# A decoder layer on one core: the second feed-forward's first product by seven quarter products per tile

## The chip, the cores and the metric

The kernel runs on one core of a Trainium2 chip. The metric is the time of one execution on the device in microseconds (us). Before the change it is 1444.54 us, the median of 3 runs (1444.05 to 1444.94).

## The reference

One decoder layer for 512 tokens of width 1024, in fp32. The change touches its last line alone:

```python
def swiglu_ffn(h, w_in, w_out):
    a, b = jnp.split(h @ w_in, 2, axis=-1)
    return (jax.nn.silu(a) * b) @ w_out

x = x + 0.5 * swiglu_ffn(rmsnorm(x, ffn1_norm_g), ffn1_w_in, ffn1_w_out)
# h = rmsnorm(x); sparse attention, gated convolution and attention into 256 memory tokens;
# their gated sum through a product with w_out is added to x
x = x + 0.5 * swiglu_ffn(rmsnorm(x, ffn2_norm_g), ffn2_w_in, ffn2_w_out)
```

The inner width is 2816, so w_in is 1024 x 5632 and w_out 2816 x 1024.

## The kernel before, in words

x is held transposed, xT: 8 blocks of 128 features on the partitions, 512 tokens in the columns. TensorE multiplies in fp32r. To keep fp32's accuracy every operand is split into a high and a low half, and each product is three matmuls into one PSUM bank, hi*hi, lo*hi and hi*lo (`mm3`, L237). In the feed-forward the 128 x 128 weight block is the stationary operand and 512 tokens move.

Stages: the first feed-forward, the attention, convolution and memory stages, the product with w_out of the layer, then the second feed-forward (`tail`, L1204, calls `ffn`, L301). `ffn` goes through 22 tiles of 128 inner features. A tile is two units of 24 matmuls (8 blocks of x by three), one for a into bank "g", one for b into "o". VectorE (DVE) and ScalarE (ACT) apply the token scale R = 1/rms, since x goes into the product unnormalized, then the gate: tanh on ACT, the rest on DVE, and split the result into ghi and glo. After 8, 15 and 22 tiles come eight units with w_out, which add into xT.

`Weights` (L95) delivers the weights. A unit is at most 128 x 1024; SP issues its transfer into one of three `wraw` buffers, and ACT (L130, cast to hi) and DVE (L131, the remainder lo) split it in two halves, each half ahead of its use. A raw buffer is free when its second half is split, and then SP issues the next transfer. Each engine takes its instructions in the order of its own queue. The order in the code is the program's, and a scheduler at build time moves instructions of DVE, ACT and PE within their dependences, and chooses which free buffer a tile gets.

Of the kernel before, what the change touches and what calls it, by code (L numbers as in the profile page):

```python
# [23 lines left out]
FFN_GROUPS = ((0, 8), (8, 15), (15, 22))  # L24
# [6 lines left out]
RAW_BUFS = 3  # L31
LINE = 256
PAD_LEFT, PAD_RIGHT = 128, 224
LOOK = 1
# [8 lines left out]
TOK["w"] = (256, (4, 4))  # L43

# [49 lines left out]

class Weights:  # L95


    def __init__(self, nc, pool, units):
        self.nc, self.pool, self.units = nc, pool, units
        self.i = self.i_dma = self.i_split = 0  # L100
        self.raw, self.parts = {}, {}

    def _dma(self, part=None):
        j = self.i_dma
        ap, _ = self.units[j]
        if part != 1:
            n = ap.shape[1]
            self.raw[j] = (self.pool.tile([128, 1024], F32, tag="wraw", name=f"wraw{j}", bufs=RAW_BUFS), n)
        t, n = self.raw[j]
        c = slice(0, n) if part is None else slice(512 * part, 512 * part + 512)  # L110
        self.nc.sync.dma_start(t[:, c], ap[:, c])
        if part != 0:
            self.i_dma += 1

    def _half(self):

        j = self.i_split
        t, n = self.raw[j]
        if j not in self.parts:
            hi = self.pool.tile([128, 1024], F32R, tag="whi", name=f"whi{j}", bufs=LOOK + 1)  # L120
            lo = self.pool.tile([128, 1024], F32R, tag="wlo", name=f"wlo{j}", bufs=LOOK + 1)
            self.parts[j] = (hi, lo)
            c = slice(0, min(n, 512))
        else:
            c = slice(512, n)
        if c.stop == n:
            self.raw.pop(j)
            self.i_split += 1
        hi, lo = self.parts[j]
        self.nc.scalar.copy(hi[:, c], t[:, c])  # L130
        self.nc.vector.tensor_sub(lo[:, c], t[:, c], hi[:, c].bitcast(F32))  # L131
        self.prefetch()

    def prefetch(self):
        while self.i_dma < len(self.units) and self.i_dma < self.i_split + RAW_BUFS:
            self._dma()

    def use(self, key):

        assert self.units[self.i][1] == key, (self.units[self.i][1], key)  # L140
        self.prefetch()
        while self.i_split <= self.i:
            self._half()
        self.i += 1
        self.ahead()
        return self.parts[self.i - 1]

    def ahead(self):

        self.parts.pop(self.i - 2, None)  # L150
        if self.i_split < len(self.units) and self.i_split <= self.i + LOOK - 1:
            self._half()


class Layer:
    def __init__(self, ctx, tc, ins, out, dbg=None):
# [10 lines left out]
        self.ws = Weights(nc, self.wp, self.unit_list())  # L167
# [16 lines left out]
    def unit_list(self):  # L184
        i = self.ins
        u = []

        def ffn(n):
            for gi, (f0, f1) in enumerate(FFN_GROUPS):
                for f in range(f0, f1):  # L190
                    for ab in range(2):
                        u.append((i[f"w{n}i"][f, ab], (n, "in", f, ab)))
                for m in range(NK):
                    u.append((i[f"w{n}o"][m][:, f0 * 128:f1 * 128], (n, "out", gi, m)))

        ffn("f1")
        for c in range(4):
            for q in range(4):
                u.append((i["wmkv"][c, q], ("mkv", c, q)))
        def tok(n, qs):  # L200
            for q in qs:
                u.append((i["t" + n][q][:, :TOK[n][0] * TOK[n][1][q]], ("tok", n, q)))

        def w1(kind, qs):
            for q in qs:
                u.append((i["w1" + "kv"[kind]][q], ("w1", kind, q)))
# [12 lines left out]
        u.append((i["w2k"], ("w2", 0)))  # L219
# [4 lines left out]
        u.append((i["w2v"], ("w2", 1)))  # L224
# [3 lines left out]
        for p in range(8):  # L228
            for t in range(6):
                u.append((i["wfeat"][p, t], ("feat", p, t)))  # L230
        for m in range(NK):
            u.append((i["wout"][m], ("wout", m)))
        ffn("f2")
        return u
# [66 lines left out]
    def ffn(self, key, pool, xhi, xlo, R, done, before, extra=()):  # L301
# [3 lines left out]
        nc = self.nc  # L305
        ghi = pool.tile([128, 8, 512], F32R, tag="ghi", name=self.nm("ghi"))
        glo = pool.tile([128, 8, 512], F32R, tag="glo", name=self.nm("glo"))
        def up(f, ab):
            whi, wlo = self.ws.use((key, "in", f, ab))
            p = self.ps("go"[ab])  # L310
            for k in range(NK):
                if k == NK // 2:
                    self.ws.ahead()
# [13 lines left out]
        for gi, (f0, f1) in enumerate(FFN_GROUPS):  # L327
            nf = f1 - f0
            for f in range(f0, f1):
                p = up(f, 0)  # L330
                if f > 0:
                    a = act_a(p)
                p2 = up(f, 1)
                if f == 0:
                    before()
                    a = act_a(p)
                nc.vector.tensor_tensor(a, a, p2, op=ALU.mult)  # L337
                self.split(ghi[:, f - f0], glo[:, f - f0], a)
                if 0 < f <= len(extra):
                    extra[f - 1]()  # L340
            for m in range(NK):
                whi, wlo = self.ws.use((key, "out", gi, m))
                p = self.ps("s")
                for k in range(nf):
                    if k == NK // 2:
                        self.ws.ahead()
                    c = slice(k * 128, (k + 1) * 128)
                    self.mm3(p, whi[:, c], wlo[:, c], ghi[:, k], glo[:, k], k == 0, k == nf - 1)
                if gi < len(FFN_GROUPS) - 1:
                    nc.vector.scalar_tensor_tensor(self.xT[:, m], p, 0.25, self.xT[:, m], op0=ALU.mult, op1=ALU.add)  # L350
                else:
                    done(m, p)


    def run(self):
# [41 lines left out]
        for k in range(NK):  # L397
            self.split_scaled(self.Ahi[:, k], self.Alo[:, k], self.xT[:, k], self.small[:, C_G1 + k:C_G1 + k + 1])
            if k in (0, 3):
                self.ws._half()  # L400
# [15 lines left out]
        self.ffn("f1", fp, self.Ahi, self.Alo, R, x1_done, x_rstd,  # L416
# [142 lines left out]
    def tok_chunk(self, c, evac):  # L559
# [4 lines left out]
        def quantum(q, tb):  # L564
# [4 lines left out]
            elif tb == 2:  # L569
                self.ws.ahead()  # L570
# [11 lines left out]
    def stage_b(self, memkv, prep, kfin):  # L582
# [20 lines left out]
        def evac_qm(half):  # L603
            def f(tb, p):
                nc.scalar.copy(mtok[:, tb, half * 512:half * 512 + 512], p)
                for h in (2 * half, 2 * half + 1):
                    sq = m1.tile([128, 256], F32, tag="qsq", name=self.nm("qsq"))
                    nc.scalar.activation(sq, mtok[:, tb, h * 256:(h + 1) * 256], AF.Square,
# [150 lines left out]
    def compress(self, cp, kcv, kind):  # L759
# [69 lines left out]
        def second():  # L829
            p = self.ps("t")  # L830
            hhi, hlo = st["h"]
            whi, wlo = (w.rearrange("p (k c) -> p k c", k=8) for w in self.ws.use(("w2", kind)))
# [371 lines left out]
    def tail(self, mx1):  # L1204
# [11 lines left out]
        f2 = ExitStack()  # L1216
        fp = self.pool(f2, "fp2", "left")
        xhi = fp.tile([128, NK, S], F32R, name="x2hi")
        xlo = fp.tile([128, NK, S], F32R, name="x2lo")
        acc = fp.tile([128, 512], F32, tag="acc", name="acc3")  # L1220
        for m in range(NK):
# [8 lines left out]
            self.prep_post(fp, m, self.xT[:, m], C_G2, xhi, xlo, acc)  # L1230
# [7 lines left out]

        def y_done(m, p):
            y = fp.tile([128, 512], F32, tag="y", name=self.nm("y"), bufs=2)  # L1240
# [3 lines left out]
        self.ffn("f2", fp, xhi, xlo, R, y_done, x_rstd)  # L1244
# [83 lines left out]
```

## Time and profile before

| | |
|---|---|
| median of 3 runs | 1444.54 us |
| profiled execution | 1445.14 us |
| its span, first to last instruction | 1443.4 us |
| PE busy | 1431.8 us (99%), 6915 matmuls |
| DVE busy | 887.8 us (62%) |
| ACT busy | 631.5 us (44%) |
| second feed-forward on PE | 1078.72 to 1439.5 us of the span |

PE is TensorE's matmuls, PEld its weight loads. Times inside the trace count from the span's start. Busy times of PE are overlapped: a matmul's shown duration is longer than its distance from the next one, so the length of a run of matmuls is read from starts.

### The profile page before, as it was taken

Reading aid. Unit: us, or ns where it says so; the run is one execution under the profiler, and the core shown is the slowest. Engines: PE = TensorE matmul, PEld = TensorE weight load, DVE = VectorE, ACT = ScalarE, POOL = GpSimd, SP = SyncE. Lnnn points to the kernel's source line nnn. Section 1 sums busy time; section 2 is a strip of 40 time slices with the busy share of each in tenths; the row PEclk is TensorE's granted clock in tenths of the full one; section 3 lists DMA queues with packets and bytes.
Section 4 is the critical chain, followed back from the end, with each engine's and each line's share of the span. In section 5 each row is a group of like instructions: output and inputs, shape, how many; then the busy total and the mean of one; then the engine's idle time right before and its main releaser. Section 6 shows DMA issues by size and latency. Waiting matters only on the chain.

```text
span 1443.4 us, 18864 instructions
## 1 busy us (share of the span) xinstructions
PE 1431.8 (99%) x6915; PEld 1198.8 (83%) x6915; DVE 887.8 (62%) x2120; ACT 631.5 (44%) x1455; POOL 1.3 (0%) x8
## 2 busy tenths in 40 slices
PE   9999999999999999999999999999999999999998
PEld 7888888888888789888888888888888888888887
DVE  7463554554766576678887887887665543543543
ACT  5242232233556645565655666565543322322331
POOL 0000000000000000000000000000000000000000
PEclk9999999999999999999999999999999999999999
DMA  5733333333452431222222222222233333333332
GB/s 179 247 123 102 97 87 101 97 96 91 149 169 92 125 94 59 89 94 68 74 75 80 67 82 74 66 74 74 73 93 97 90 100 101 90 90 110 91 93 97
DMA packets 42892, 142.62 MB, mean 99 GB/s; under 512 B 4704, under 2 KB 4992, under 8 KB 42672
## 3 DMA queue, kind: packets, MB, share of 16 engines
q1 hardware_dynamic: 40320, 134.83, 30.0%
q10 hardware_dynamic: 2480, 6.60, 1.3%
q8 instruction: 54, 0.88, 0.3%
q14 instruction: 38, 0.31, 0.1%
HBM read 139.27 MB, written 7.51 MB: 102 GB/s over the span
## 4 chain that ended last, share of the span: by engine, by line
PE 97%; DVE 1%; ACT 1%; DMA 0%; issue 0%; SPq 0%; ACTq 0%
PE psg L240 15%; PE psg L241 15%; PE psg L242 15%; PE pso L240 8%; PE pso L242 8%; PE pso L241 8%; PE pss L241 6%; PE pss L242 6%; PE pss L240 6%; PE pst L1044 2%; PE pso L1068 1%; PE pss L1002 1%; PE pss L1001 1%; PE pso L1067 1%; PE pst L969 1%; DMA xT<-xT 0%
## 5 line engine op out<-in xcount | busy, mean ns | idle before, releaser
L130 ACT CAST whi<-wraw 128x512 fp32r<-128x512 f32 (+1 forms) x492 | 279.5, 609 | 564.9 <-issue 324.1
L131 DVE TENSOR_TENSOR wlo<-wraw,whi 128x512 fp32r<-128x512 f32 (+1 forms) x492 | 315.1, 674 | 68.6 <-ACT whi L130 68.0
L240 PE MATMUL psg<-Ahi,whi 128*128 128x512 f32 x624 | 247.6, 397 | 0.5 <-ACT Ahi L278 0.3
L241 PE MATMUL psg<-Alo,whi 128*128 128x512 f32 x624 | 244.3, 392 | 1.2 <-DVE Alo L279 1.0
L242 PE MATMUL psg<-Ahi,wlo 128*128 128x512 f32 x624 | 243.8, 391 | 0.0
L242 PEld LDWEIGHTS psg<-Ahi,wlo 128*128 128x128 f32 x624 | 117.1, 188 | 25.2
L240 PE MATMUL pss<-ghi,whi 128*128 128x512 f32 x352 | 137.0, 389 | 0.0
L242 PE MATMUL pss<-ghi,wlo 128*128 128x512 f32 x352 | 136.9, 389 | 0.0
L241 PE MATMUL pss<-glo,whi 128*128 128x512 f32 x352 | 136.9, 389 | 0.0
L241 PEld LDWEIGHTS psg<-Alo,whi 128*128 128x128 f32 x624 | 117.4, 188 | 23.5 <-DVE Alo L279 2.6
L240 PEld LDWEIGHTS psg<-Ahi,whi 128*128 128x128 f32 x624 | 117.3, 188 | 23.1 <-ACT Ahi L278 1.3
L978 ACT ACTIVATE P<-P,nm 128x128 f32<-128x128 f32 (+3 forms) x128 | 72.0, 563 | 83.1 <-DVE nm L977 82.2
L321 DVE TENSOR_TENSOR fa<-psg,R 128x512 f32<-128x512 f32 x44 | 30.4, 691 | 120.7 <-PE psg L242 117.9
L350 DVE SCALAR_TENSOR_TENSOR xT<-pss,xT 128x512 f32<-128x512 f32 x32 | 22.1, 691 | 100.6 <-PE pss L242 100.6
L337 DVE TENSOR_TENSOR fa<-fa,pso 128x512 f32<-128x512 f32 x44 | 30.2, 687 | 86.9 <-PE pso L242 86.9
L282 ACT CAST PThi<-pst 128x512 fp32r<-128x512 f32 (+3 forms) x128 | 54.4, 425 | 58.2 <-PE pst L1044 57.8
L241 PEld LDWEIGHTS pss<-glo,whi 128*128 128x128 f32 x352 | 66.1, 188 | 13.8
L242 PEld LDWEIGHTS pss<-ghi,wlo 128*128 128x128 f32 x352 | 66.1, 188 | 13.8
L240 PEld LDWEIGHTS pss<-ghi,whi 128*128 128x128 f32 x352 | 66.1, 188 | 13.6
L283 DVE TENSOR_TENSOR PTlo<-pst,PThi 128x512 fp32r<-128x512 f32 (+3 forms) x128 | 62.2, 486 | 21.4 <-ACT PThi L282 21.2
L977 DVE CUSTOM_DVE_ANT_0 P<-pss,T 128x128 f32<-128x128 f32 (+3 forms) x128 | 61.9, 483 | 16.4 <-PE pss L1002 16.4
L242 PE MATMUL pso<-Ahi,wlo 128*128 128x512 f32 x176 | 68.6, 390 | 0.0
(291 smaller groups left out, 2741.8 us busy)
## 6 DMA issues: line engine op xcount, KB each, us to landing
wraw<-wfeat SPq DMA_DIRECT2D x48, 512.0 KB, 3.5
wraw<-wf2i SPq DMA_DIRECT2D x44, 512.0 KB, 3.6
wraw<-wf1i SPq DMA_DIRECT2D x43, 512.0 KB, 3.6
wraw<-wmkv SPq DMA_DIRECT2D x16, 512.0 KB, 3.4
wraw<-wf1o SPq DMA_DIRECT2D x16, 448.0 KB, 3.3
wraw<-wf2o SPq DMA_DIRECT2D x16, 448.0 KB, 3.4
scr<-scr ACTq DMA_DIRECT2D x1, 5248.0 KB, 27.4
T<-scr SPq DMA_DIRECT2D x16, 264.0 KB, 3.4
```

The lines of the kernel that those rows point to most:

```text
L130: self.nc.scalar.copy(hi[:, c], t[:, c])
L131: self.nc.vector.tensor_sub(lo[:, c], t[:, c], hi[:, c].bitcast(F32))
L240: mm(ps, ahi, bhi, start=start, stop=False)
L241: mm(ps, ahi, blo, start=False, stop=False)
L242: mm(ps, alo, bhi, start=False, stop=stop)
L282: self.nc.scalar.copy(hi, src)
L283: self.nc.vector.tensor_tensor(lo, src, hi.bitcast(F32), op=ALU.subtract)
L321: nc.vector.tensor_tensor(a, p, R, op=ALU.mult)
L337: nc.vector.tensor_tensor(a, a, p2, op=ALU.mult)
L977: self.nc.vector.tensor_tensor_reduce(P, s, T, -0.125, 3.0e38, ALU.add, ALU.min, nm)
L978: self.nc.scalar.activation(P, P, AF.Exp, scale=-1.0, bias=nm, accum_out=ssum)
L1044: nc.tensor.transpose(p[:, (i - j) * 128:(i - j + 1) * 128], P[:, o:o + 128], self.ident)
```

## The change

Tiles 0 to 3 of the second feed-forward stay as they are. For each of tiles 4 to 21 the two units (a and b, 128 features each, over 1024 features of x and 512 tokens) are seen as one product of 2 x 2 by 2 x 2 quarters: the weights' quarters are a or b by the lower or upper 512 features of x, x's quarters are lower or upper features by tokens 0 to 255 or 256 to 511. Strassen's scheme in Winograd's form gives the four results by seven quarter products P1 to P7 instead of eight. Each is 4 feature blocks by three matmuls, with 256 tokens moving.

The sums of weight quarters (S1 to S4) are made by DVE for each tile from both raw units, before the split into halves; those of x's quarters once, while tiles 1 to 3 run. x is normalized first, so that R is not applied later. Results are summed in PSUM where they can be: P2 onto P1's bank, P6, P5 and P3 onto a copy of P1 in bank "o" (an ACT copy), P4 onto P7. ACT keeps two intermediate sums (u2, s7), DVE adds them.

The units with w_out come in six groups of 4, 4, 4, 4, 3 and 3 tiles and are placed one by one between the products. For the whole kernel, halves of weights are tiles of their own (six instead of four), raw buffers are five instead of three, and the split may run three halves ahead of use. The first feed-forward keeps its groups and steps.

The order of one tile on PE is P1, P7, P3 of the tile before, a w_out unit, P6, P2, P4, a w_out unit, P5; tiles 7 and 8 have none or one.

```diff
-FFN_GROUPS = ((0, 8), (8, 15), (15, 22))
+FFN_GROUPS = {1: ((0, 8), (8, 15), (15, 22)), 2: ((0, 4), (4, 8), (8, 12), (12, 16), (16, 19), (19, 22))}
+
+FAST = {"P1": "A11", "P2": "A12", "P3": "S4", "P4": "A22", "P5": "S1", "P6": "S2", "P7": "S3"}
...
-RAW_BUFS = 3
+RAW_BUFS = 5
+RING = 6
 LINE = 256
 PAD_LEFT, PAD_RIGHT = 128, 224
-LOOK = 1
+LOOK = 3
...
+def ffn_steps(n):
+
+    groups = FFN_GROUPS[n]
+    out = []
+    if n == 1:
+        for g, (f0, f1) in enumerate(groups):
+            out += [("up", f) for f in range(f0, f1)] + [("down", g, m) for m in range(NK)]
+        return out
+    f0, f1 = groups[0]
+    out += [("up", f) for f in range(f0, f1)]
+    downs = [("down", 0, m) for m in range(NK)]
+    starts = {g[0]: k for k, g in enumerate(groups)}
+
+    def down(k):
+        out.extend(downs[:k])
+        del downs[:k]
+
+    for f in range(f1, NF):
+        out.append(("prod", f, "P1"))
+        if f == f1:
+            down(2)
+        out.append(("prod", f, "P7"))
+        if f > f1:
+            out.append(("prod", f - 1, "P3"))
+            down(1)
+        out += [("prod", f, "P6"), ("prod", f, "P2")]
+        down(1 if f == f1 else 0)
+        out.append(("prod", f, "P4"))
+        if starts.get(f, 0) >= 2:
+            down(len(downs))
+            downs += [("down", starts[f] - 1, m) for m in range(NK)]
+        down(1)
+        out.append(("prod", f, "P5"))
+    out.append(("prod", NF - 1, "P3"))
+    down(len(downs))
+    return out + [("down", len(groups) - 1, m) for m in range(NK)]
...
+    def add_fast(self, a, b, f, name):
+
+        if name == "P1":
+            self.fast = getattr(self, "fast", {})
+            self.fast[f] = (len(self.units), len(self.units) + 1)
+            self.units += [a, b]
+        j = self.fast[f]
+        free = {"P2": j[:1], "P4": j[1:]}.get(name, ())
+        self.specs.append((("prod", f, name), 512, FAST[name], j, None, free))
...
+    def prefetch(self):
+        while self.i_free in self.freed:
+            self.i_free += 1
+        while self.i_dma < len(self.units) and self.i_dma < self.i_free + RAW_BUFS:
+            self._dma()
+
+    def _sum(self, name, j, x, y, op):
+        t = self.sum_pool.tile([128, 512], F32, tag="sum" + name, name=f"sum{name}_{j}")
+        self.nc.vector.tensor_tensor(t, x, y, op=op)
+        self.sums[name, j] = t
+        return t
+
+    def _source(self, kind, js, c):
+        if kind == "raw":
+            return self.raw[js[0]][:, c]
+        j = js[0]
+        if kind in ("S1", "S4"):
+            return self.sums.pop((kind, j))
+        lo, hi = slice(0, 512), slice(512, 1024)
+        a, b = self.raw[js[0]], self.raw[js[1]]
+        if kind == "A11":
+            return a[:, lo]
+        if kind == "A12":
+            return a[:, hi]
+        if kind == "A22":
+            return b[:, hi]
+        if kind == "S3":
+            return self._sum("S3", j, a[:, lo], b[:, lo], ALU.subtract)
+        self._sum("S1", j, b[:, lo], b[:, hi], ALU.add)
+        return self._sum("S2", j, self.sums["S1", j], a[:, lo], ALU.subtract)
+
+    def _make(self):
+
+        i = self.made
+        key, width, kind, js, c, free = self.specs[i]
+        src = self._source(kind, js, c)
+        w = src.shape[1]
+        hi = self.pool.tile([128, 512], F32R, tag="whi", name=f"whi{i}", bufs=RING)
+        lo = self.pool.tile([128, 512], F32R, tag="wlo", name=f"wlo{i}", bufs=RING)
+        self.nc.scalar.copy(hi[:, :w], src)
+        self.nc.vector.tensor_sub(lo[:, :w], src, hi[:, :w].bitcast(F32))
...
+        if kind == "A12":
+            self._sum("S4", js[0], src, self.sums.pop(("S2", js[0])), ALU.subtract)
+        self.parts[i] = (hi, lo)
+        self.made += 1
+        self.freed.update(free)
         self.prefetch()
 
-    def prefetch(self):
-        while self.i_dma < len(self.units) and self.i_dma < self.i_split + RAW_BUFS:
-            self._dma()
+    def ahead(self):
+
+        if self.made < min(len(self.specs), self.taken + LOOK):
+            if self.sum_pool or self.specs[self.made][2] in ("raw", "A11"):
+                self._make()
...
+        while self.taken < len(self.specs) and self.specs[self.taken][0] == key:
+            while self.made <= self.taken:
+                self._make()
+            self.taken += 1
+        p = [self.parts.pop(i) for i in range(i0, self.taken)]
         self.ahead()
-        return self.parts[self.i - 1]
-
-    def ahead(self):
-
-        self.parts.pop(self.i - 2, None)
-        if self.i_split < len(self.units) and self.i_split <= self.i + LOOK - 1:
-            self._half()
+        return tuple(Columns([x[n] for x in p], self.specs[i0][1]) for n in range(2))
...
+        def prod(f, name):
+            s = st.setdefault(f, {})
+            whi, wlo = ws.use(("prod", f, name))
+            xh, xl = forms[name]
+            if name == "P1":
+                s["A"], s["B"], s["E"] = self.ps("g"), self.ps("o"), self.ps("t")
+            p = s[{"P1": "A", "P2": "A", "P7": "E", "P4": "E"}.get(name, "B")][:, :256]
+            for k in range(4):
+                c = slice(k * 128, (k + 1) * 128)
+                for i, (w, x) in enumerate(((whi, xh), (whi, xl), (wlo, xh))):
+                    nc.tensor.matmul(p, w[:, c], x[:, k], start=k == 0 and i == 0 and name in ("P1", "P7"),
+                                     stop=k == 3 and i == 2, skip_group_check=True)
+            small = lambda t: late["p"].tile([128, 256], F32, tag=t, name=self.nm(t), bufs=2)
+            wide = lambda t: pool.tile([128, 512], F32, tag=t, name=self.nm(t), bufs=2)
+
+            def gate(h):
+                th = small("th")
+                nc.scalar.activation(th, p, AF.Tanh, scale=0.5)
+                nc.vector.scalar_tensor_tensor(s["a"][:, h], th, 1.0, p, op0=ALU.add, op1=ALU.mult)
+
+            h0, h1 = slice(0, 256), slice(256, 512)
+            if name == "P1":
+                nc.scalar.copy(s["B"][:, :256], p)
+            elif name == "P7":
+                s["s7"] = small("s7")
+                nc.scalar.copy(s["s7"], p)
+            elif name == "P6":
+                s["u2"] = small("u2")
+                nc.scalar.copy(s["u2"], p)
+            elif name == "P2":
+                s["a"] = wide("fa")
+                gate(h0)
+            elif name == "P4":
+                s["b"] = wide("fth")
+                nc.vector.tensor_tensor(s["b"][:, h0], p, s["u2"], op=ALU.add)
+            elif name == "P5":
+                nc.vector.tensor_tensor(s["b"][:, h1], p, s["s7"], op=ALU.add)
+            else:
+                gate(h1)
+                nc.vector.tensor_tensor(s["a"], s["a"], s["b"], op=ALU.mult)
+                put(f, s["a"])
+                del st[f]
+            more()
...
+            if gi < len(groups) - 1:
+                nc.vector.scalar_tensor_tensor(self.xT[:, m], p, 0.25, self.xT[:, m], op0=ALU.mult, op1=ALU.add)
+            else:
+                done(m, p)
+            if forms:
+                more(2)
...
+            square_sum(m)
...
+        B = {(i, j): xn[:, 4 * i:4 * i + 4, 256 * j:256 * j + 256] for i in range(2) for j in range(2)}
+        T = {}
+
+        def norm(k):
+            nc.vector.scalar_tensor_tensor(xn[:, k], self.xT[:, k], self.small[:, C_G2 + k:C_G2 + k + 1], R,
+                                           op0=ALU.mult, op1=ALU.mult)
+
+        def diff(name, x, y):
+            T[name] = quarter()
+            nc.vector.tensor_tensor(T[name], T.get(x, B.get(x)), T.get(y, B.get(y)), op=ALU.subtract)
+
+        def parts(name, x):
+            self.split(*forms[name], T.get(x, B.get(x)))
...
+        prep = [lambda k=k: norm(k) for k in range(NK)] + [
+            lambda: parts("P1", (0, 0)), lambda: diff("T3", (1, 1), (0, 1)), lambda: parts("P7", "T3"),
+            lambda: diff("T1", (0, 1), (0, 0)), lambda: diff("T2", (1, 1), "T1"), lambda: parts("P5", "T1"),
+            lambda: parts("P6", "T2"), lambda: parts("P2", (1, 0)), lambda: diff("T4", (1, 0), "T2"),
+            lambda: parts("P4", "T4"), lambda: (parts("P3", (1, 1)), fs.close())]
...
+        self.ffn(2, fp, xhi, xlo, R, y_done, x_rstd, prep, forms, plain_done)
```

On PE, in the second feed-forward before, at the change from the a unit (psg) to the b unit (pso) of one plain tile:

```order
L240 MATMUL psg_1101_10614<-x2hi_9820,whi191_10574 128x512
L241 MATMUL psg_1101_10614<-x2lo_9821,whi191_10574 128x512
L242 MATMUL psg_1101_10614<-x2hi_9820,wlo191_10575 128x512
L240 MATMUL pso_1104_10653<-x2hi_9820,whi192_10610 128x512
L241 MATMUL pso_1104_10653<-x2lo_9821,whi192_10610 128x512
L242 MATMUL pso_1104_10653<-x2hi_9820,wlo192_10611 128x512
```

On PE, after, the end of P3 of tile 5 (Ahi and Alo hold a quarter of x there) and the start of a w_out unit behind it:

```order
L471 MATMUL pso_1151_11144<-Ahi_78,whi395_11309 128x256
L471 MATMUL pso_1151_11144<-Alo_79,whi395_11309 128x256
L471 MATMUL pso_1151_11144<-Ahi_78,wlo395_11310 128x256
L345 MATMUL pss_1170_11404<-ghi_1114_10654,whi396_11326 128x512
L346 MATMUL pss_1170_11404<-glo_1115_10655,whi396_11326 128x512
L347 MATMUL pss_1170_11404<-ghi_1114_10654,wlo396_11327 128x512
```

A plain tile has 48 matmuls of 512 columns (8 times the first three rows, then 8 times the last three), a tile of products 84 of 256 columns (7 times 4 times the first three rows of the second excerpt).

On DVE before, one plain tile: its gate and, between, the low halves of the coming units (wlo):

```order
L321 TENSOR_TENSOR fa_1102_10643<-psg_1101_10614,R3_10133 128x512
L131 TENSOR_TENSOR wlo193_10650<-wraw193_10554,whi193_10649 128x512 x2
L323 SCALAR_TENSOR_TENSOR fa_1102_10643<-fth_1103_10644,fa_1102_10643 128x512
L324 TENSOR_TENSOR fa_1102_10643<-fa_1102_10643,R3_10133 128x512
L337 TENSOR_TENSOR fa_1102_10643<-fa_1102_10643,pso_1104_10653 128x512
L131 TENSOR_TENSOR wlo194_10686<-wraw194_10593,whi194_10685 128x512 x2
L283 TENSOR_TENSOR glo_1071_10135<-fa_1102_10643,ghi_1070_10134 128x512
```

On DVE after, around the change from tile 13 (wraw222 and wraw223) to tile 14 (wraw226 and wraw227); wraw224 and wraw225 are w_out units:

```order
L228 TENSOR_TENSOR wlo456_12576<-wraw224_12462,whi456_12575 128x512
L516 SCALAR_TENSOR_TENSOR xT_77<-pss_1250_12544,xT_77 128x512
L228 TENSOR_TENSOR wlo457_12600<-sumS2_222_12597,whi457_12599 128x512
L497 TENSOR_TENSOR fth_1249_12536<-pso_1239_12393,s7_1241_12428 128x256
L228 TENSOR_TENSOR wlo458_12618<-wraw222_12297,whi458_12617 128x512
L196 TENSOR_TENSOR sumS3_226_12725<-wraw226_12484,wraw227_12623 128x512
L228 TENSOR_TENSOR wlo459_12646<-wraw223_12436,whi459_12645 128x512
L228 TENSOR_TENSOR wlo460_12668<-wraw225_12464,whi460_12667 128x512
L228 TENSOR_TENSOR wlo461_12688<-sumS1_222_12595,whi461_12687 128x512
L479 SCALAR_TENSOR_TENSOR fa_1247_12516<-th_1255_12637,pso_1239_12393 128x256
```

DVE's rows per tile go from nine of 512 columns (low halves counted singly) to 17 of 512 and four of 256 with two w_out units among them. By the addresses of the built program wraw227 takes the space of wraw224, which the first row of the last excerpt reads last, and the sum S3 of tile 14 is the first to read wraw227.

## Rows read from the trace of the kernel before

**Rows 1.** The page: busy time by engine; granted clock in 40 slices.

```profile
PE 1431.8 (99%) x6915; PEld 1198.8 (83%) x6915; DVE 887.8 (62%) x2120; ACT 631.5 (44%) x1455; POOL 1.3 (0%) x8
...
PEclk9999999999999999999999999999999999999999
```

**Rows 2.** Windows: the second feed-forward; columns: length, busy by engine, clock, DMA.

```profile
1078.70:1439.50 360.80, 360.77 (x1597) 298.31 (x1595) 169.82 (x282) 100.03 (x181) 0.00 (x0) 1.00 0.32 96
```

**Rows 3.** Waits in that stretch: total us, times, longest.

```profile
ACT whi L130 <- PE pss L241: 74.5, 19, 4.3
DVE fa L321 <- PE psg L242: 60.1, 20, 3.5
...
PEld pst L273 <- DVE line_fp L254: 0.3, 1, 0.3
```

**Rows 4.** Timeline, PE: first matmul of two neighbouring units; start, duration.

```profile
1078.72 0.39 PE L240 MATMUL psg<-x2hi,whi 128*128 128x512 f32 x1
...
1084.16 0.39 PE L240 MATMUL pso<-x2hi,whi 128*128 128x512 f32 x1
```

**Rows 5.** Timeline, PE: first and last of two runs of twelve 256-column matmuls.

```profile
467.43 0.28 PE L240 MATMUL pss<-whi,cohi 128*128 128x256 f32 x1
...
468.75 0.28 PE L242 MATMUL pss<-whi,colo 128*128 128x256 f32 x1
...
532.13 0.28 PE L240 MATMUL pss<-KmT,mqh 128*128 128x256 f32 x1
...
533.43 0.28 PE L242 MATMUL pss<-KmT,mql 128*128 128x256 f32 x1
```

**Rows 6.** Timeline, DVE: neighbours without a wait.

```profile
390.31 1.41 DVE L429 SCALAR_TENSOR_TENSOR hn<-xT,small,R 128x512 f32<-128x512 f32 x2
...
506.81 0.42 DVE L810 SCALAR_TENSOR_TENSOR cs<-cth,pss 128x256 f32<-128x256 f32 x1
507.15 0.17 DVE L252 TENSOR_TENSOR line_m<-line_m 128x16 f32<-128x16 f32 x1
...
1097.10 0.68 DVE L321 TENSOR_TENSOR fa<-psg,R 128x512 f32<-128x512 f32 x1
1097.70 0.68 DVE L324 TENSOR_TENSOR fa<-fa,R 128x512 f32<-128x512 f32 x1
1098.30 0.68 DVE L131 TENSOR_TENSOR wlo<-wraw,whi 128x512 fp32r<-128x512 f32 x1
```

**Rows 7.** Timeline, ACT: casts of 512 columns, an operation of 256.

```profile
384.25 0.42 ACT L516 ACTIVATE ksq<-km 128x256 f32<-128x256 f32 x1
384.57 0.18 ACT L516 ACTIVATION_READ_ACCUMULATOR ksq<-km 128x1 f32 x1
...
1183.60 1.14 ACT L130 CAST whi<-wraw 128x512 fp32r<-128x512 f32 x2 [4.30 <-PE pss L241]
```

**Rows 8.** Timeline, DVE and SP: release and issue; landing of wraw, 1150 to 1440.

```profile
1189.88 1.28 DVE L131 TENSOR_TENSOR wlo<-wraw,whi 128x512 fp32r<-128x512 f32 x2
...
1191.19 5.76 SPq L111 DMA_DIRECT2D wraw<-wf2i  x2
...
DMA to landing us min/median/max: 3.2/3.5/5.5
```

**Rows 9.** Timeline: first use of R; start of tile 5's b unit.

```profile
1095.10 0.69 DVE L321 TENSOR_TENSOR fa<-psg,R 128x512 f32<-128x512 f32 x1 [1.36 <-ACT R L274]
...
1140.11 0.39 PE L240 MATMUL pso<-x2hi,whi 128*128 128x512 f32 x1
```

**Rows 10.** Windows: the stages between the first feed-forward and the attention rounds.

```profile
420.00:610.00 190.00, 186.01 (x1051) 160.80 (x1050) 117.50 (x293) 102.39 (x243) 0.50 (x2) 1.00 0.30 95
```

**Rows 11.** Timeline, PEld: weight loads of 256-column matmuls.

```profile
523.31 0.19 PEld L240 LDWEIGHTS pss<-KmT,mqh 128*128 128x128 f32 x1
523.42 0.19 PEld L241 LDWEIGHTS pss<-KmT,mqh 128*128 128x128 f32 x1
523.54 0.19 PEld L242 LDWEIGHTS pss<-KmT,mql 128*128 128x128 f32 x1
```

More of the change, by code (lines that the diff above doesn't have):

```diff
@@ new lines, with __init__, add @@
+class Weights:
+    def __init__(self, nc, pool):
+        self.nc, self.pool = nc, pool
+        self.units, self.specs = [], []
+        self.i_dma = self.i_free = self.made = self.taken = 0
+        self.raw, self.parts, self.freed = {}, {}, set()
+        self.sum_pool, self.sums = None, {}
+    def add(self, ap, key, width=512):
+        j, n = len(self.units), ap.shape[1]
+        self.units.append(ap)
+        for c0 in range(0, n, width):
+            c1 = min(c0 + width, n)
+            self.specs.append((key, width, "raw", (j,), slice(c0, c1), (j,) if c1 == n else ()))
+    def add_fast(self, a, b, f, name):
[6 more added lines that the diff above has]
+        self.specs.append((("prod", f, name), 512, FAST[name], j, None, free))
@@ L298, in square_sum, with ffn, more, half_up @@
             nc.vector.tensor_tensor(acc, acc, sq[:, :src.shape[1]], op=ALU.add)
[L301 to L309, printed above, removed]
+    def ffn(self, n, pool, xhi, xlo, R, done, before, extra=(), forms=None, plain_done=None):
+        nc, ws = self.nc, self.ws
+        groups = FFN_GROUPS[n]
+        extra = list(extra)
+        g, st, late = {}, {}, {}
+        def more(k=1):
+            for fn in extra[:k]:
+                fn()
+            del extra[:k]
+        def half_up(f, ab):
+            whi, wlo = ws.use((n, "in", f, ab))
             p = self.ps("go"[ab])
@@ L325, in act_a, with put @@
             return a
-        for gi, (f0, f1) in enumerate(FFN_GROUPS):
-            nf = f1 - f0
[L329 to L352, printed above, removed]
+        def put(f, a):
+            g[f] = tuple(pool.tile([128, 512], F32R, tag="g" + x, name=self.nm("g" + x), bufs=8) for x in ("hi", "lo"))
+            self.split(*g[f], a)
@@ new lines, in up @@
+        def up(f):
+            p = half_up(f, 0)
+            if f > 0:
+                a = act_a(p)
+            if forms and f:
+                more()
+            p2 = half_up(f, 1)
+            if f == 0:
+                before()
+                a = act_a(p)
+            nc.vector.tensor_tensor(a, a, p2, op=ALU.mult)
+            put(f, a)
+            if f:
+                more()
+        def prod(f, name):
[38 more added lines that the diff above has]
+                del st[f]
+            more()
@@ L355, in run @@
+        steps = ffn_steps(n)
+        for step, after in zip(steps, steps[1:] + [(None,)]):
+            {"up": up, "prod": prod, "down": down}[step[0]](*step[1:])
+            if step[0] == "up" and after[0] == "prod":
+                late["p"] = ws.sum_pool = plain_done()
+                ws.ahead()
+        assert not extra
     def run(self):
```

144 lines of the change are left out of this document (83 added, 61 removed).

## The prediction

> **What bounds the kernel now.** I read the page's first two parts, then the second feed-forward's stretch, then who waits there. TensorE (PE) is busy for 99% of the span, in nearly every slice, at a granted clock of 1.00, the upper of its two levels, 2.4 GHz [rows 1]. In the second feed-forward its busy time is the stretch itself, 360.77 of 360.80 us [rows 2]; there VectorE (DVE) and ScalarE (ACT) wait for PE, and PE for nobody [rows 3]. So this stretch is as long as PE's instructions, and DVE has half of its time free (169.82 us busy [rows 2]). A matmul's duration (389 ns) overlaps the next one's; what counts is the distance of starts. One unit of 24 matmuls with 512 moving columns, from the first psg to the first pso matmul, takes 1084.16 - 1078.72 = 5.44 us: 0.2267 us each [rows 4].
>
> **Part 1, what leaves PE.** Tiles 4 to 21 lose the two plain units of 24 matmuls: 18 x 48 = 864, at 0.2267 us 195.9 us.
>
> **Part 2, what comes to PE.** Each of the 18 tiles has seven products of 4 x 3 matmuls with 256 columns: 18 x 84 = 1512. The trace has such matmuls back to back in the middle of the kernel: twelve of them start in 468.75 - 467.43 = 1.32 us and in 533.43 - 532.13 = 1.30 us [rows 5], over 11 distances 0.120 and 0.118 us. I take 0.119: 1512 x 0.119 = 179.9 us. PE so gains 195.9 - 179.9 = **16.0 us**, between 14.5 (at 0.120) and 17.5 (at 0.118). In columns the change saves an eighth; in time it saves a twelfth, since half the columns take 0.52 of the time. The other units of the product with w_out (22 x 8 x 3 matmuls) stay, in six groups.
>
> The Trainium skill, "TensorE: Matmul & The Clock Gate", section "Back-to-back issue gap", gives N/2.4 + 2.5 ns for N columns at full clock. By it I would have 215.8 and 109.2 ns, and a gain of 186.5 - 165.1 = 21.4 us. The rows show 226.7 and 119, so the trace's 16.0 stands.
>
> **Part 3, what comes to DVE and whether it hides.** A steady tile with two w_out units (most of tiles 9 to 18) has on DVE 17 operations of 512 columns: four sums of weight quarters, nine low halves (seven products, two w_out units), one gating product, one split, two accumulations into xT; and four of 256 columns. Back to back, a 512-column operation starts 0.60 us after the one before, a 256-column one takes 0.34 [rows 6]: 17 x 0.60 + 4 x 0.34 = 11.6 us. PE needs 84 x 0.119 + 24 x 0.2267 = 15.4 us for the same tile. ACT has ten casts at 0.52 us (1.14 for two that overlap) and five 256-column operations at about 0.32 [rows 7]: 6.8 us. Both hide behind PE on average.
>
> The place where DVE can be held is in the second DVE excerpt of the change: S3 of tile 14 needs wraw227, whose transfer goes into the space of wraw224, free only after the subtraction four rows earlier. On the way stand an accumulation, two subtractions and one 256-column addition, 3 x 0.60 + 0.34 = 2.1 us. The queue issues a transfer 0.03 us after the release (1189.88 + 1.28 = 1191.16, issue 1191.19), and it lands 3.5 us later, at most 5.5 [rows 8]. So DVE would stand for some 3.6 - 2.1 = 1.5 us, with all behind it on its engine queued (A22 and S1 subtractions, the gate of the tile before). That makes DVE's round 11.6 + 1.5 = 13.1 us, and 15.1 with the latest landing, still under PE's 15.4. If DVE is late once, PE notices only after about 2.4 us: P3 of a tile writes the bank that DVE reads after P5, and P3 comes two products (2.9 us) after P5, less some 0.5 us for that read; the weights themselves stand 4 us and more ahead. Cost of this part: 0.3 us, bounds 0 and 7 (0.6 us over PE's round in about twelve tiles with the wait).
> In the stretch without w_out units (tile 7 and most of 8) DVE has 13 x 0.60 + 4 x 0.34 = 9.2 us against 84 x 0.119 = 10.0, and S3 of tile 8 stands 11 rows behind its release: nothing.
>
> **Part 4, the way in.** Before tile 4 DVE must make the normalized x, its sums and splits. From R on (1095.10 [rows 9]) until the gating product of tile 3 its queue holds 34 operations of 512 columns, eight of them normalizations at 0.66 (1.41 for two [rows 6]), and eight of 1024 columns, which no row shows; 256 columns more cost 0.26, so I take 0.60 + 2 x 0.26 = 1.12. Sum 34 x 0.60 + 8 x 0.06 + 8 x 1.12 = 29.9 us, to 1125.0; the split of tile 3 (0.69 + 0.62 + 0.69 and handovers) ends at 1127.1. PE reaches tile 4 three units before 1140.11 [rows 9], at 1123.8, does P1 (1.4 us) and needs that split in the tenth matmul of the next unit, at 1127.5. It just fits. I put 0.5 us on it; 0 to 3 if a 1024-column operation costs up to 1.4.
> R's multiplications go (two per tile on DVE, off the path). The end is as before: the last accumulation, 0.69 us, and an output transfer.
>
> **Part 5, the rest of the kernel.** The weight pipeline (six half buffers for four, five raw buffers for three, up to three specs ahead) reorders ACT and DVE everywhere. Elsewhere PE is without gaps except for 4.0 us in 420 to 610 [rows 10] and the start. More lookahead can give back about half of that, a worse order there can cost as much: 0, bounds -2 and +2.
>
> **Sum.** -16.0 + 0.3 + 0.5 + 0 = -15.2 us. The profiled execution took 1445.14 us (span 1443.4 and 1.7 around it), 0.6 above the median of the runs; 1445.14 - 15.2 - 0.6 = **1429.3 us**. The bounds that go together leave 1426.5 to 1435.
>
> **Rivals.**
> (a) *DVE becomes the clock in part.* Between a weight sum and its low half stands an ACT cast. If the three such round trips of a tile (S3, S2, the split of g) were exposed, 3 x 0.72 = 2.2 us come on 13.1: 15.3, and any further lateness goes to PE. With 0.8 us over PE's round in twelve tiles, 9.6 - 2.4 = 7.2 us of the gain go: 1436.5. For it: one in-order queue carries it all. Against: in the DVE order ten other rows stand between S3 or S2 and its low half, and two (1.2 us) between the gating product and the split's low half.
> (b) *The same, at its worst: slower.* Exposed round trips and landings of 5.5 us make 13.1 + 2.0 + 2.2 = 17.3 us: 1.9 x 12 - 2.4 = 20 us of stalls in tiles 6 to 21, and 1449. It decides against the change from a DVE round of 16.9 us on (15.4 + 17.6 / 12). Against: only the maximum of the landings is 5.5, the median is 3.5 [rows 8].
> (c) *Weight loads set the pace.* A load takes 0.19 us [rows 11], more than the 0.119 that I count on; in a run of 84 that could come through: 1512 x 0.188 = 284 us, 88 more than before, 1533. It decides from 195.9 / 1512 = 0.130 us on. Against: the loads of [rows 11] start every 0.12 us, each while the one before is under way. A smaller excess in long runs, 0.125, would give 1438.5.
> The Trainium skill, same page, "Part 3: Packing small matmuls", "The mechanism", has loads overlap running matmuls only where the row groups differ. That would speak for (c). These rows, full 128 x 128 tiles, overlap nonetheless, so I give it little.
> (d) *The products wait for each other*, through copies from bank to bank (P1 into P6's bank): one exposed wait of 0.4 us per tile is 7 us, 1436.5. Against: two products or more lie between each such pair.
>
> **How the numbers follow.** Forecast 0.70, (a) 0.12, (b) 0.05, (c) in full 0.03, in part 0.05, (d) 0.05. Its own range is 1426.5 to 1435; 1426 to 1440 takes in (d), the smaller (c) and most of (a), and leaves out (b), the full (c) and the deep end of (a), some 0.15. A difference of 0.2% (2.9 us) is about what a measurement of this kernel can tell from none: a quarter of (a), two fifths of the smaller (c) and a fifth of (d), each at its dear end, fall within it, 0.06. Slower are (b) and the full (c), 0.08. Faster is the rest, 0.86.
>
> **What would show it.** The second feed-forward's stretch on PE some 345 us long, PE still busy throughout; 1512 matmuls of 256 columns 0.119 us apart, in the middle of a run as in rows 5; no row of PE waiting for whi, wlo or a bank by more than 1 us in total; DVE 75 to 85% busy there, with one wait of 1 to 2 us per tile for wraw before S3. A distance of 0.125 or more, or PE gaps at P3 or P7 that come back every tile, would make it wrong.

## The result and the profile after

The kernel after takes 1425.8 us (median, 1425.58 to 1426.05), 18.7 less than the 1444.47 of before; the ratio is 0.9871 [0.9854, 0.9888]. The forecast was 1429.3 us, 15.2 less, with a range from 1426.0 to 1440: the direction held, and the time lies 0.2 us below the range.

The page after, first line and clock, answers [rows 1]; PE is as busy as before, in a span of 1424.2 us for 1443.4:

```profile
PE 1416.7 (99%) x7563; PEld 1217.5 (85%) x7563; DVE 1001.9 (70%) x2309; ACT 711.6 (50%) x1590; POOL 1.3 (0%) x8
...
PEclk9999999999999999999999999999999999999999
```

The windows after of the second feed-forward and of 420 to 610 us answer [rows 2, 10] (length, then busy time of PE, PEld, DVE, ACT, POOL, then granted clock, DMA share and GB/s):

```profile
1073.20:1420.50 347.30, 347.24 (x2245) 317.33 (x2244) 273.22 (x467) 160.56 (x311) 0.00 (x0) 1.00 0.31 95
420.00:610.00 190.00, 189.79 (x1073) 164.55 (x1072) 123.35 (x311) 106.59 (x250) 0.56 (x2) 1.00 0.29 95
```

PE has next to no gap in either: the second has 0.2 us of idle time where before had 4.0 [rows 10]. Where the time went is read from starts. The last matmul of before, and the first and the last of the second feed-forward after (timeline, PE):

```profile
1439.09 0.39 PE L242 MATMUL pss<-ghi,wlo 128*128 128x512 f32 x1
```

```profile
1073.24 0.39 PE L345 MATMUL psg<-x2hi,whi 128*128 128x512 f32 x1
...
1420.05 0.39 PE L347 MATMUL pss<-ghi,wlo 128*128 128x512 f32 x1
```

With the first matmul of before at 1078.72 [rows 4] the stretch took 360.37 us before and 346.81 after: **-13.56**, where -15.2 was forecast. And it starts **5.48 us earlier**, where 0 was forecast. What lies behind the last matmul is 0.2 us shorter. Together -19.2, the difference of the two spans.

The 5.48 us come before the second feed-forward. Of before, then of after, the same two instructions (first product with cohi, first low-half product with chh of 64 columns):

```profile
459.19 0.36 PE L240 MATMUL pss<-whi,cohi 128*128 128x256 f32 x1
...
511.81 0.27 PE L241 MATMUL pst<-wlo,chh 128*128 128x64 f32 x1
```

```profile
459.26 0.36 PE L345 MATMUL pss<-whi,cohi 128*128 128x256 f32 x1
...
507.25 0.28 PE L346 MATMUL pst<-wlo,chh 128*128 128x64 f32 x1
```

52.62 us before, 47.99 after: 4.63 of the 5.48. A second place is at 616 us, where PE waits for qn (1.0 us before, 0.5 after). The view of waits, PE alone, whole program, before and after (total, times, longest):

```profile
PE psg L240 <- ACT whi L130: 1.7, 2, 1.2
PE pst L383 <- DVE zero L380: 1.1, 1, 1.1
PE psg L241 <- DVE Alo L279: 1.0, 3, 0.5
PE pst L969 <- DVE qn L959: 1.0, 1, 1.0
PE psg L241 <- DVE wlo L131: 0.9, 1, 0.9
PE pss L240 <- ACT whi L130: 0.9, 2, 0.5
...
PE pss L241 <- DVE wlo L131: 0.3, 1, 0.3
```

```profile
PE pst L559 <- DVE zero L556: 1.1, 1, 1.1
PE psg L346 <- DVE Alo L384: 1.0, 3, 0.5
PE psg L345 <- ACT Ahi L383: 0.8, 1, 0.8
PE pst L1145 <- DVE qn L1135: 0.5, 1, 0.5
```

The waits for weight halves (whi, wlo), 3.8 us in six places of before, are gone. They are listed with less than they cost. At 468.75 a matmul of before starts [rows 5], and the next one, of the same program place in all kernels here, is:

```profile
470.25 0.50 PE L240 MATMUL psg<-whi,Ahi 128*128 128x512 f32 x1 [1.23 <-ACT whi L130]
```

The idle time shown is 1.23 us, the distance of the starts 1.50; without the wait it is 0.12 (after: 467.55 to 467.67). The wait costs 1.38 us. A matmul's shown duration runs beyond its successor's usual start, and idle time is counted from that end, so such a wait is shown too short and a short one not at all.

### The profile page after: what moved, and what is told of

It is laid out like the page before. It is cut to its first block, busy times and chain, and to the rows that moved or that the text cites. A ratio compares the mean times of both kernels' runs of the same rounds, so it can differ in the third digit from the quotient of the medians.

```text
span 1424.2 us, 20852 instructions
## 1 busy us (share of the span) xinstructions
PE 1416.7 (99%) x7563; PEld 1217.5 (85%) x7563; DVE 1001.9 (70%) x2309; ACT 711.6 (50%) x1590; POOL 1.3 (0%) x8
## 4 chain that ended last, share of the span: by engine, by line
PE 97%; DVE 1%; ACT 1%; DMA 0%; issue 0%; SPq 0%; ACTq 0%
PE psg L345 13%; PE psg L346 13%; PE psg L347 13%; PE pss L345 6%; PE pss L346 6%; PE pss L347 6%; PE pso L347 5%; PE pso L345 5%; PE pso L471 5%; PE pso L346 5%; PE psg L471 4%; PE pst L471 4%; PE pst L1220 2%; PE pso L1244 1%; PE pss L1178 1%; PE pss L1177 1%
## 5 line engine op out<-in xcount | busy, mean ns | idle before, releaser
L227 ACT CAST whi<-wraw 128x512 fp32r<-128x512 f32 (+3 forms) x476 | 286.6, 609 | 380.0 <-PE pss L346 112.5
L228 DVE TENSOR_TENSOR wlo<-wraw,whi 128x512 fp32r<-128x512 f32 (+3 forms) x476 | 317.9, 674 | 172.5 <-ACT whi L227 169.2
L227 ACT CAST whi<-sumS 128x512 fp32r<-128x512 f32 x72 | 44.6, 621 | 65.5 <-PE pss L346 27.8
L1153 DVE CUSTOM_DVE_ANT_0 P<-pss,T 128x128 f32<-128x128 f32 (+3 forms) x128 | 61.8, 483 | 15.4 <-PE pss L1178 15.2
L346 PE MATMUL pso<-Alo,whi 128*128 128x512 f32 x176 | 68.5, 389 | 0.0
L345 PE MATMUL pso<-Ahi,whi 128*128 128x512 f32 x176 | 68.5, 389 | 0.0
```

What stands on the lines that cost most here:

```text
L227: self.nc.scalar.copy(hi[:, :w], src)
L228: self.nc.vector.tensor_sub(lo[:, :w], src, hi[:, :w].bitcast(F32))
L345: mm(ps, ahi, bhi, start=start, stop=False)
L346: mm(ps, ahi, blo, start=False, stop=False)
L1153: self.nc.vector.tensor_tensor_reduce(P, s, T, -0.125, 3.0e38, ALU.add, ALU.min, nm)
```

## The experiments

Each was timed in five rounds beside the kernel before (medians 1444.32 to 1444.48). "Stretch" is the distance from the first to the last matmul of the second feed-forward in the trace (before 360.37, after 346.81), "start" the time of the first, and "459 to 512" the distance of the two instructions shown above (first with cohi, first low-half one with chh of 64 columns). Profiled executions differ by up to about 1 us in their first 460 us (with five half buffers by more, see below), so a start alone is good to 1 us.

| kernel | time, us | ratio to before | 459 to 512 | start | stretch |
|---|---|---|---|---|---|
| before | 1444.47 | 1 | 52.62 | 1078.72 | 360.37 |
| after | 1425.80 | 0.9871 [0.9854, 0.9888] | 47.99 | 1073.24 | 346.81 |
| pipeline alone | 1438.62 | 0.9961 [0.9947, 0.9975] | 47.96 | 1072.17 | 360.34 |
| after, 4 half buffers and 2 halves ahead | 1431.82 | 0.9912 [0.9898, 0.9925] | 54.27 | 1078.77 | 346.95 |
| after, 5 half buffers | 1431.94 | 0.9913 [0.9900, 0.9927] | 52.28 | 1078.65 | 346.74 |
| after, 3 raw buffers up to the last stage | 1425.84 | 0.9871 [0.9857, 0.9884] | 47.97 | 1073.00 | 346.81 |
| after, 2 halves ahead up to the last stage | 1425.76 | 0.9870 [0.9854, 0.9885] | 48.01 | 1072.89 | 346.81 |
| 4 half buffers, short squares on ACT | 1430.26 | 0.9903 [0.9889, 0.9916] | 50.93 | 1076.37 | 346.94 |
| pipeline alone, matmuls cut in two | 1451.02 | 1.0045 [1.0033, 1.0058] | 48.01 | 1073.48 | 371.92 |
| after, 3 more DVE additions a tile | 1425.42 | 0.9868 [0.9854, 0.9882] | 47.98 | 1073.20 | 346.82 |
| after, 8 more DVE additions a tile | 1444.11 | 0.9999 [0.9990, 1.0008] | 47.97 | 1073.03 | 365.12 |
| after, w_out units in pairs | 1425.33 | 0.9866 [0.9852, 0.9880] | 47.97 | 1072.27 | 346.54 |

**The pipeline alone.**

```diff
-FFN_GROUPS = {..., 2: ((0, 4), (4, 8), (8, 12), (12, 16), (16, 19), (19, 22))}
+FFN_GROUPS = {..., 2: ((0, 8), (8, 15), (15, 22))}
-    if n == 1:
+    if n:
```

(and `tail` as before.) 

> The kernel before with the new weight pipeline alone (five raw buffers, six half buffers, up to three halves ahead); the second feed-forward in plain units and its old groups. Theory A (the pipeline gave the gain that I had put at 0): the part up to the second feed-forward is as in the kernel after, so its start on PE falls from 1078.7 to 1073.2 us and the time from 1444.5 to 1439.0 us (-5.5). Rival B (the gain outside came with the products, for instance by transfers or space of the second feed-forward): 1443.5 to 1445.

5.9 us less than before, the stretch unchanged. Up to the second feed-forward the order on PE, ACT and DVE is that of the kernel after, so theory A holds and B is out: some 5.5 us of the gain have nothing to do with the products.

**Which part of it: half buffers, raw buffers, or how far ahead.** The first edit takes two numbers back, since four half buffers go with two halves ahead; each of the others changes one:

```diff
-RING = 6
-LOOK = 3
+RING = 4
+LOOK = 2
```

> The kernel after with four half buffers for six and two halves ahead for three; five raw buffers stay. Theory A1 (the casts waited for a free half buffer, and the buffers' number took that wait away): the waits of PE in 459 to 516 us come back, the second feed-forward starts at 1077 to 1079 us, and the time is 1429.5 to 1431. Rival A2 (the raw buffers did it): start at 1073 to 1074, time 1426 unless the second feed-forward itself suffers from four buffers.

```diff
-self.i_free + RAW_BUFS
+self.i_free + self.nraw     # 3; 5 from the product with the layer's w_out on
```

> The kernel after with three raw buffers for five until the product with the layer's w_out, then five; the order of the instructions on PE, ACT and DVE up to there is the same. Theory A1 (half buffers): start of the second feed-forward at 1073.2 to 1073.8, time 1425.8 to 1426.5. Rival A2 (raw buffers, transfers that land earlier): the casts wait for transfers in 459 to 516 us, start at 1077 to 1079, time 1430 to 1431.

```diff
-self.taken + LOOK
+self.taken + self.look      # 2; 3 from the product with the layer's w_out on
```

> The kernel after with the split at most two halves ahead for three until the product with the layer's w_out, then three; six half buffers and five raw buffers stay. Theory (the number of half buffers alone): 1425.5 to 1426.1, start of the second feed-forward at 1073 to 1074 us. Rival (the third half ahead is a part of it): 1428 to 1431.

```diff
-RING = 6
+RING = 5
```

> The kernel after with five half buffers for six. Theory (a stock of split halves carries PE over a burst on ACT, so every buffer counts): the waits of PE in 459 to 516 us come back in part, by one half's matmuls (12 x 0.227 = 2.7 us) per burst at most: time 1427 to 1430, between the 1425.8 of six and the 1431.8 of four. Rival (five suffice; four fail since a unit's two halves and the next one's two fill them all): 1425.5 to 1426.2.

Three raw buffers and two halves ahead change nothing (1425.84, 1425.76). With four half buffers the start is back at that of before and the stretch stays: 6.0 us lost, ahead of the second feed-forward. So the half buffers gave the 5.5 us: the two halves ahead that the first edit also has cost nothing by themselves. (With their number the scheduler's order ahead of that stage changes too, 60 rows' lines on PE; with three raw buffers it is the same, with two halves ahead the same but for two lines on DVE.) With five the time missed my range: five are as slow as four. The profile with five shows two waits of PE for weights (timeline, PE):

```profile
62.88 0.50 PE L347 MATMUL pso<-Ahi,wlo 128*128 128x512 f32 x1 [1.53 <-DVE wlo L228]
...
473.10 0.99 PE L345 MATMUL psg<-whi,Ahi 128*128 128x512 f32 x2 [2.94 <-ACT whi L227]
```

The second is the wait that four buffers have, six matmuls of the unit later, and 459 to 512 takes 52.28 us for their 54.27. So the fifth buffer does give 2.0 us there. The first stands in the first feed-forward, where neither four nor six show one; up to the first matmul with cohi this profile is 1.8 us later than that of four. That takes the gain back. Why the wait at 62.88 comes, and whether every run has it, is not shown.

**Why PE waited there.** In the kernel with four, at the place shown above (timeline, PE; then ACT):

```profile
467.89 0.28 PE L347 MATMUL pss<-whi,colo 128*128 128x256 f32 x1
471.29 0.60 PE L345 MATMUL psg<-whi,Ahi 128*128 128x512 f32 x1 [3.12 <-ACT whi L227]
```

```profile
462.37 1.15 ACT L227 CAST whi<-wraw 128x512 fp32r<-128x512 f32 x2
464.19 0.62 ACT L387 CAST cohi<-cop 128x512 fp32r<-128x512 f32 x1 [0.66 <-DVE cop L966]
464.84 0.59 ACT L781 COPY mtok<-psg 128x512 f32<-128x512 f32 x1
...
470.55 0.19 ACT L784 ACTIVATION_READ_ACCUMULATOR qsq<-mtok 128x1 f32 x1
470.64 0.60 ACT L227 CAST whi<-wraw 128x512 fp32r<-128x512 f32 x1
```

No weights are cast between 463.5 and 470.6: ACT waits 0.66 us and then works without a gap on three casts of cohi, four copies and six sums of squares (the expectation below counted two and eight). The kernel after has the same burst, and its next cast comes no earlier: 12.3 us behind the first matmul with cohi with four, five and six half buffers alike. Of the kernel after (timeline, ACT; then PE):

```profile
463.31 1.15 ACT L227 CAST whi<-wraw 128x512 fp32r<-128x512 f32 x2
...
471.57 0.60 ACT L227 CAST whi<-wraw 128x512 fp32r<-128x512 f32 x1
```

```profile
467.67 0.40 PE L345 MATMUL psg<-whi,Ahi 128*128 128x512 f32 x1
```

Yet its PE goes on at 467.67, since the halves for the next unit were made before the burst.

With four, the wait costs more than its own length. Windows of that kernel behind it (the clock is the third number from the end):

```profile
472.00:473.00 1.00, 1.00 (x4) 0.71 (x4) 1.00 (x4) 1.00 (x5) 0.00 (x0) 0.50 0.00 0
473.00:474.00 1.00, 1.00 (x4) 0.81 (x3) 1.00 (x3) 1.00 (x3) 0.00 (x0) 0.50 0.20 20
...
475.00:476.00 1.00, 1.00 (x6) 0.78 (x6) 0.01 (x1) 0.00 (x0) 0.00 (x0) 1.00 0.81 328
```

PE stood, and the granted clock behind that is 0.50, the lower of its two levels, 1.2 GHz: eleven matmuls from 471.29 to 475.51 take 4.22 us, where 11 x 0.2267 are 2.49. With five it is the same, nine matmuls in 3.75 us for 2.04. In the kernels before and after it stays at 1.00 from 455 to 512. So four buffers lose 3.3 us by the wait (3.40 from start to start, less 0.12) and 1.7 by the clock at this place; before lost its 4.63 at full clock, most of it in six short waits. That both kernels start the second feed-forward at 1078.7 is partly chance.

To test whether the burst is what holds the cast, the kernel with four buffers was given shorter squares:

```diff
-nc.scalar.activation(sq[:, :256], mtok[:, tb, h * 256:(h + 1) * 256], ...
+nc.scalar.activation(sq[:, :32], mtok[:, tb, h * 256:h * 256 + 32], ...
```

> The kernel with four half buffers, in which the 16 sums of squares of the memory queries on ACT (256 columns each) take 32 columns in place of 256, so these norms are not the reference's. In the kernel with four buffers ACT works without a gap from 464.2 to 470.6 us on eight of them, four copies and two casts, and PE waits 3.1 us for the next weights' cast behind them. Theory (that burst holds the cast): eight times some 0.25 us less, the wait falls to some 1 us and the time by 2 us, to 1429.5 to 1430.5. Rival (the cast waits for its buffer, not for ACT's turn): 1431.5 to 1432.

```profile
469.69 0.50 PE L345 MATMUL psg<-whi,Ahi 128*128 128x512 f32 x1 [0.73 <-ACT whi L227]
```

The wait fell from 3.12 to 0.73 us (with one more of 0.73 for wlo behind it), 459 to 512 from 54.27 to 50.93 and the start by 2.4 us (good to 1); the granted clock stays at 1.00 there. The median time fell by 1.6, which is not clear of the noise: the intervals of both ratios overlap, its four runs took 1429.28, 1429.29, 1431.22 and 1432.15 us, and the profile shows one of the first two. (The scheduler also put the cast a few rows earlier, between the squares; both free it from the burst, and the run does not tell them apart.) So, by the trace, it is ACT's turn that the cast waits for, not a buffer, and the two more half buffers are stock that covers the burst.

**What 256 columns cost.** In the pipeline-alone kernel:

```diff
+if n == 2 and f >= 4:      # 864 matmuls of 512 columns as 1728 of 256
+    for t in (slice(0, 256), slice(256, 512)):
+        ... nc.tensor.matmul(p[:, t], w[:, c], x[:, k, t], ...)
```

> The pipeline-only kernel with the 864 matmuls of tiles 4 to 21 each cut into two of 256 columns (1728), no products. If 256 columns cost 0.120 us in every run: 1728 x 0.120 - 195.9 = +11.5 us over the pipeline-only kernel. At the 0.119 that the prediction took: +9.7. If long runs are set by the weight loads (0.125): +20.

The time rose by 12.4 us, the stretch by 371.92 - 360.34 = 11.58. That is 0.120 us for each (11.5), with 384 and twice 672 such matmuls in a row, and neither 0.119 nor the slower pace of the weight loads that I had as a rival.

**How much VectorE could bear.**

```diff
+for _ in range({"P7": 1, "P2": 1, "P5": 1}.get(name, 0)):     # or eight a tile
+    z = late["p"].tile([128, 512], F32, tag="z", ...)
+    nc.vector.tensor_tensor(z, self.xT[:, 0], self.xT[:, 1], op=ALU.add)
```

> The kernel after with three more additions of 512 columns on VectorE in each tile of products (after P7, P2 and P5; their result goes nowhere). Theory (PE sets the pace; a tile with two w_out units takes PE 15.6 us and VectorE 11.6 us of work, so 1.8 us more fits): 1425.6 to 1427. Rival (VectorE's waits for ACT's casts take what is left, so it stands at the edge): 1430 or more.

> The kernel after with eight such additions per tile. Theory: VectorE's work is 11.6 + 4.8 = 16.4 us against PE's 15.6 in a tile with w_out units, 0.8 over in some 13 tiles, less 2.4 of slack, and 9.2 + 4.8 = 14.0 against 10.1 in the two tiles without: +8 and +6, so 1436 to 1444 (with VectorE's waits up to 1450). Rival (VectorE far from the clock, the casts of ACT or the banks set the slack): under 1430.

Windows of 1200 to 1300 us: after, with three, with eight (busy time of PE, PEld, DVE):

```profile
1200.00:1300.00 100.00, 100.00 (x695) 93.61 (x694) 78.26 (x136) 48.07 (x97) 0.00 (x0) 1.00 0.32 96
```

```profile
1200.00:1300.00 100.00, 100.00 (x695) 93.61 (x695) 90.07 (x158) 48.08 (x97) 0.00 (x0) 1.00 0.33 96
```

```profile
1200.00:1300.00 100.00, 97.27 (x658) 89.40 (x657) 100.00 (x178) 45.26 (x94) 0.00 (x0) 1.00 0.32 96
```

Three are free: PE keeps its 695 matmuls. Eight make VectorE the clock and eat the gain, 18.3 us, at the upper edge of what was expected. The shown idle time is short again: PE's busy share falls by 2.7%, its matmuls by 5.3%.

**The w_out units in pairs.**

```diff
 out.append(("prod", f - 1, "P3"))
-down(1)
+down(2)                    # and from tile 8 on none behind P4
```

> The kernel after with a tile's two w_out units one behind the other (behind P3) and not one behind P3 and one behind P4; some 18 changes between 256 and 512 columns in place of 36. In the trace of after the twelve 512-column matmuls behind products take 0.03 us more than twelve in a plain run. If that belongs to the change of width: 0.5 us less, 1425.2 to 1425.6; VectorE's accumulations then come in pairs, and a rival is that PE then waits for VectorE: 1427 or more.

The stretch is 0.27 us shorter, with 22 changes of width in place of 36; 1425.33 is the lowest median here, but the intervals of both ratios overlap, and the start of this profile is 1 us early. As a better version it is not shown.

## Why the prediction was wrong, point by point

**The step that failed is part 5**, "the rest of the kernel": "More lookahead can give back about half of that, a worse order there can cost as much: 0, bounds -2 and +2". It gave 5.5 us. I had read 4.0 us of idle time for 420 to 610 [rows 10], and taken half of it for the bound without looking at the single waits. Two errors lie in it. Nearly all of it went, not half. And idle time is less than what a wait costs: the 52.62 us of before shrank by 4.63, while PE's listed waits for weights were 3.8. Had I gone through PE's six waits for whi and wlo, each of which the change's larger ring addresses, the bound would have been some -5, and the range would have held the time. The low bounds that stand in the prediction, -17.5 for the products and -2 here, give 1425.0 together, below the time; the range left them out as not going together.

**Part 1 and 2, the products,** were right in kind, and PE sets the pace as forecast. The size was off by 2.5 us, in two terms. The 1512 matmuls took 0.1198 us, not 0.119: the starts behind them add to 181.2 us, 1.3 more than forecast (0.120 was one of the two rows, and I took the mean). And the matmuls of 512 columns behind a run of 256 are a little slower. One w_out unit of four tiles and the two products after it (timeline, PE, after):

```profile
1203.33 0.40 PE L345 MATMUL pss<-ghi,whi 128*128 128x512 f32 x1
...
1206.08 0.28 PE L471 MATMUL pso<-xP5hi,whi 128*128 128x256 f32 x1
...
1211.83 0.40 PE L345 MATMUL pss<-ghi,whi 128*128 128x512 f32 x1
```

Twelve of 512 take 2.75 us, where 12 x 0.2267 are 2.72; with 36 such units, some 1.2 us in all. The other 48 take 5.75, 0.1198 each. -16.0 + 1.3 + 1.2 = -13.5, which is the stretch's -13.56. The two stalls that I had added (0.3 and 0.5) did not come.

**Part 3, VectorE behind PE,** was right: 273.22 us busy of 347.3, 79%, between the 75 and 85 forecast, and PE waits for nothing of it. The mechanism that I feared, a stand of 1.5 us per tile at S3, was wrong. In one tile of the kernel after (timeline, DVE; then SP):

```profile
1251.23 0.68 DVE L228 TENSOR_TENSOR wlo<-wraw,whi 128x512 fp32r<-128x512 f32 x1
1252.96 0.69 DVE L516 SCALAR_TENSOR_TENSOR xT<-pss,xT 128x512 f32<-128x512 f32 x1 [1.04 <-PE pss L347]
1253.57 0.68 DVE L228 TENSOR_TENSOR wlo<-sumS,whi 128x512 fp32r<-128x512 f32 x1
...
1256.00 0.69 DVE L196 TENSOR_TENSOR sumS<-wraw,wraw 128x512 f32<-128x512 f32 x1 [0.33 <-issue]
```

```profile
1251.94 0.33 SPq L184 DMA_DIRECT2D wraw<-wf2i  x1
```

The release, the issue 0.03 us later and the four rows are as forecast. But between them VectorE waits for PE (1.04 us, for the w_out unit), since it runs up against PE and not back to back, and the landing hides in that wait; 0.33 us are left here. Of the 18 tiles only one other shows a wait before S3, of 0.66 us. I had lined up VectorE's rows as if it were the late one. So rivals (a) and (b) had no ground: VectorE's slack is over 1.8 us a tile, and it becomes the clock below 4.8, as the two runs with additions show.

**Part 4, the way in,** fitted as closely as forecast. A 1024-column operation takes 1.14 us on VectorE (1.12 estimated), and tile 3's split ends 0.1 us ahead of its reader (timeline after, DVE, then PE):

```profile
1118.26 1.22 DVE L388 TENSOR_TENSOR Alo<-xn,Ahi 128x1024 fp32r<-128x1024 f32 x1
1119.40 0.68 DVE L456 TENSOR_TENSOR fa<-fa,pso 128x512 f32<-128x512 f32 x1
...
1121.20 0.69 DVE L388 TENSOR_TENSOR glo<-fa,ghi 128x512 fp32r<-128x512 f32 x1
```

```profile
1122.01 0.42 PE L346 MATMUL pss<-glo,whi 128*128 128x512 f32 x1
```

**Rival (c),** the weight loads, is out by the cut matmuls: 0.120 us with 384 and 672 in a row, with loads of 0.19 [rows 11]. The Trainium skill, "TensorE: Matmul & The Clock Gate", gives in "Back-to-back issue gap" 2.5 ns on top of N/2.4 as the gap of a matmul by itself; the prediction used it for a stream without that condition. The trace has more: 0.1198 and 0.2267 us are 13 ns above N/2.4. Its "Part 3: Packing small matmuls", "The mechanism", says in its list of what overlaps that loads overlap running matmuls only where the row groups differ; the trace disagrees here too, since full 128 x 128 tiles keep 0.120 us. (The same section also lets a load that goes to a background buffer be pulled ahead, which the trace does not contradict.) **Rival (d)** did not come: PE waits for no bank.

Two errors of opposite sign, +1.6 in the second feed-forward and -5.5 before it, with -0.2 behind it, leave the forecast 4.0 us too high in the traces and 3.5 in the medians, since the profiled runs lie above their medians by different amounts. That the time lies only 0.2 us outside the range is luck: the products gave less than forecast where the pipeline gave more.

## What to carry to other kernels

A change to a pipeline that the whole program shares is to be priced at every place where the bottleneck engine waits for it, one by one, and by the distance of starts: the idle time in the profile leaves out part of each wait. How many buffers a shared ring needed here was set by a burst of some 7 us of other work on the engine that fills it, and the place where they paid lay far from the one that they were added for. A wait of some 3 us on TensorE also brought a stretch at the lower clock here, which the view of waits does not count (1.7 us each time). And work that is cut into halves is priced at the halves' own measured pace: an eighth fewer columns were about a fifteenth less time here (13.5 of 195.9 us).

## What the runs showed of the hardware

A matmul of 256 columns starts 0.1198 us behind the one before and one of 512 columns 0.2267: 0.107 us per 256 columns and a fixed 0.013. The 0.120 us hold for 36 to 672 matmuls of 256 columns in a row. The first matmuls of 512 columns behind a run of 256 come 0.23 to 0.24 us apart. Neither cost stood in the prediction's sum; together they took 2.5 us. After a wait of 3.12 us (four half buffers) and one of 2.94 (five) TensorE's granted clock was 0.50, and matmuls of 512 columns started 0.43 us apart, for 1.7 us more in each; it came back to 1.00 while TensorE worked.
